# Four modulation vectors of the second layer: from TensorE inside the attention to ScalarE and GpSimd beside the long convolution

## The chip, the core and the metric

The program runs on one core of one Trainium2 chip, as one launch. The metric is the device time of that launch in microseconds (us), the median of the runs shown. A profile, taken in one further execution, gives the time of every instruction on every engine.

## The reference, cut to what matters

The program is a chain of two blocks on a sequence of 512 positions with 1024 features, all in float32. The first block has two layers; each is steered by six vectors of 1024 numbers that depend only on the input vector `c` and on one weight matrix per layer:

```
c_act = silu(c)                                        # 1024 numbers
for i in (0, 1):
    mod = c_act @ ada_w[i] + ada_b[i]                  # 1024 x 6144 weights
    sh1, sc1, g1, sh2, sc2, g2 = split(mod, 6)
    h = rms_norm(x, norm_mix_g[i]) * (1 + sc1) + sh1
    y = mla_mixer(h) if i == 0 else hyena_mixer(h)     # attention / long convolution
    x = x + g1 * y
    h = rms_norm(x, norm_ffn_g[i]) * (1 + sc2) + sh2
    x = x + g2 * hier_moe(h)                           # 16 experts, top 2
# second block: 2 x (retention, short conv, conformer conv, then a feed-forward)
```

The mixer of layer 1, `hyena_mixer`, is a projection to 3072 features with a three-tap convolution, and then twice a gate times a long convolution over the whole sequence (in the reference by FFT), and an output projection. Of layer 1's six vectors, `sh1` and `sc1` are needed before this mixer, and `g1`, `sh2`, `sc2` and `g2` only after it.

## The kernel before, in words

Features lie on the 128 partitions, positions along the free axis; a feature vector of 1024 is eight tiles. Matrix products run on TensorE at float32 accuracy as three products of split operands: a weight tile is loaded raw (128x1024, one DMA on SyncE's queue), ScalarE rounds it (`wh`, L257), VectorE takes the rest (`wl`, L258), and TensorE multiplies `wh` and `wl` with the activations, which are split in the same way. `fm` is the loop over such weight tiles; it hands back one output tile of 128x512 at a time.

The framework fixes the order of each engine's instructions before the launch; semaphores hold an instruction until its inputs are there, and behind it everything on that engine waits. The order follows the Python program, which interleaves generators by hand: `pump(gen, n)` lets a generator go n steps on. Generator `fill` makes modulation vectors as a filler inside the attention of layer 0 (a step after each stage of a head), beside a second filler, `filt`, which computes the filters of the long convolution.

One vector costs in `ada_vec` (L467): eight raw weight tiles through SyncE's queue; of each, four matmuls of 256 columns with `c_act` broadcast to 32 stationary columns, into the tile `ada` of a PSUM bank; then a copy on ScalarE (`adar`, L482), two transposes on TensorE (`adat`, L251), and the addition of the bias on VectorE (`mod`, L492). After layer 1's `sc2`, `router_prep(1)` follows, 16 small matmuls into the tile `rb`. `fill` is the chain of four vectors of layer 0 and all six of layer 1.

`hyena` (L1795) comes after layer 0's mixture of experts. Its first part has two loops over `fm` of eight tiles each. Per tile there are 24 matmuls into `acc`; ScalarE moves the bank out (`u`, L1687), VectorE convolves it (`y`, L1692 to L1694). In the first loop, each step also takes one of eight tiles computed earlier and put off (`late`): VectorE convolves that too and forms sums and differences of it (`eo`, L1700 and L1701), which TensorE transposes (`eoT`, L1704). The second part is the long convolution: `run` steps through forward transforms (`fwd_gen`: matmuls into `fu`, and VectorE multiplies them with the filter's spectrum `KK`, L1737 to L1745) and inverse transforms (`inv_gen`: matmuls into `iv`). GpSimd has no instruction in this whole stretch. In the trace, the first loop's convolutions with `eoT` lie between about 722 and 762 us, the second loop up to 808 us, then the first forward transform up to 829 us, and the pairs of inverse and forward transform after it.

Of the kernel before, what the change touches and what calls it, by code (L numbers as in the profile page):

```python
# [9 lines left out]
FT = mybir.dt.float32  # L10
# [3 lines left out]
AF = mybir.ActivationFunctionType  # L14
OP = mybir.AluOpType
# [7 lines left out]
KD = 8  # L23
# [430 lines left out]
ADA_OFF = {"sh1": 0, "sc1": 8, "g1": 16, "sh2": 24, "sc2": 32, "g2": 40}  # L454
# [6 lines left out]
class Mla:  # L461
# [7 lines left out]
    def ada_vec(self, i, nm):  # L469

        nc, W = self.nc, self.A["ada_w"]
        P = self.ps("ada") if (i, nm) == (0, "sh1") else self.fps("ada") if (i, nm) in EARLY else self.acc("ada")
        o = ADA_OFF[nm]
        for k in range(KD):
            raw = self.raw()
            nc.sync.dma_start(raw, W[i, k * 128:(k + 1) * 128, o * 128:o * 128 + 1024])
            c1 = self.cact[:, k:k + 1].to_broadcast([128, 32])
            for q in range(4):
                self.mm(P[32 * q:32 * q + 32, :256], c1, raw[:, 256 * q:256 * q + 256], k == 0, k == KD - 1)
            yield  # L480
        R = self.t("adar")
        nc.scalar.activation(R[:, :256], P[:, :256], AF.Copy)  # L482
        Q = self.ps("adat")
        self.tr4(Q, [R[:, b * 128:(b + 1) * 128] for b in range(2)])
        dst = self.mod[i][:, o:o + 8]
        nc.vector.tensor_tensor(
            dst.rearrange("p (q b) -> p q b", q=4),
            Q[:, :256].rearrange("p (b q z) -> p q b z", b=2, q=4)[:, :, :, 0],
            self.pc(f"ada_b{i}", o, 8).rearrange("p (q b) -> p q b", q=4), op=OP.add)
        for v, g in (("sc1", "gmix"), ("sc2", "gffn")):  # L490
            if v == nm:
                nc.vector.scalar_tensor_tensor(dst, dst, 1.0, self.pc(f"{g}{i}"), op0=OP.add, op1=OP.mult)  # L492
        yield

    def m_(self, i, nm, k):
        o = ADA_OFF[nm] + k
        return self.mod[i][:, o:o + 1]
# [382 lines left out]
class Moe:  # L880
# [301 lines left out]
    def moe_down(self, a, w, row, i):  # L1182
        if YT:
            for n in range(2):
                P, Y = self.acc("dn"), self.t("Y")
                self.down_mm(P, a, w, n)
                self.nc.scalar.activation(Y, P, AF.Copy)
                (self.nc.gpsimd, self.nc.sync, self.nc.scalar)[YQ].dma_start(
                    self.ys[i][row:row + 128, n * 512:(n + 1) * 512], Y)
            return  # L1190
        Y = self.p("Y", FT)
        for n in range(2):
            P = self.acc("dn")
            self.down_mm(P, a, w, n)
            self.nc.scalar.activation(Y[:, n * 512:(n + 1) * 512], P, AF.Copy)
        (self.nc.gpsimd, self.nc.sync, self.nc.scalar)[YQ].dma_start(self.ys[i][row:row + 128, :], Y)

# [360 lines left out]
class Hyena:  # L1558
# [236 lines left out]
    def hyena(self, norm, F, fill=None):  # L1795
        nc, A = self.nc, self.A
        rB = norm[1]
        W = A["hy_w_in"]
        EU = [self.new_eu(0) for _ in range(2)]
        H, late = [], []  # L1800

        def conv(ct, u, b):
            self.eo(self.hconv3(u, 16 + ct, b), EU[ct // 4], ct % 4)

        for ct, u in F.tiles(rB):
            late.append((ct, u, F.bias[:, ct:ct + 1]))
        for ct, u in F.more((2048 + 512, 2048 + 768), rB):
            late.append((ct + 4, u, F.bias[:, ct % 2:ct % 2 + 1]))
            for k in range(2):
                H.append(self.mod_split(len(H), rB, 1, "sc1", "sh1"))  # L1810
        F.R = None
        for c in range(2):
            for ct, P in self.fm(W, c * 1024, 1024, H):
                if late:
                    conv(*late.pop(0))
                nc.scalar.dma_start(self.xd[c, ct], self.hconv3(P, c * 8 + ct))
        del H
        self.tu, self.ti = ([self.table(A[n][a], f != m, f) for a in range(2)] for n, f, m in (("k_tu", FF, 3), ("k_ti", FI, 15)))
        Z = [None] * KD
        EU2 = [None, None]  # L1820

        def sink1(ct, z):
            if ct % 4 == 0:
                EU2[ct // 4] = self.new_eu(1)
            self.eo(z, EU2[ct // 4], ct % 4)

        def sink2(ct, z):
            Z[ct] = self.split_p(z, "z2")

        def run(*gs):  # L1830
            gs = list(gs)
            while gs:
                for g in list(gs):
                    if next(g, "end") == "end":
                        gs.remove(g)
        Y = [[] for _ in range(4)]
        run(self.fwd_gen(0, 0, EU[0], Y[0]))
        run(self.inv_gen(0, 0, Y[0], sink1), self.fwd_gen(0, 1, EU[1], Y[1]))
        run(self.inv_gen(0, 1, Y[1], sink1), self.fwd_gen(1, 0, EU2[0], Y[2]))
        run(self.inv_gen(1, 0, Y[2], sink2), self.fwd_gen(1, 1, EU2[1], Y[3]))  # L1840
        run(self.inv_gen(1, 1, Y[3], sink2))
        self.tu = self.ti = None
        if fill is not None:
            self.pump(fill, 1000)
        self.ex = 0
        return self.resid(A["hy_w_out"], Z, 1, "g1")

# [424 lines left out]
class Kernel(Base, Mla, Moe, Hyena, Mix):  # L2272

    def run(self):
        nc = self.nc
        self.startup()
        ada = self.ada_vec(0, "sc1")
        if XP0 == 0:
            self.x_load((nc.scalar, nc.sync, nc.gpsimd)[XQ])
        self.pump(ada, 3)  # L2280
        if XP0 == 1:
            self.x_load((nc.scalar, nc.sync, nc.gpsimd)[XQ])
        filt = self.filter_gen(*self.filter_consts(nc.scalar))
        if XP0 == 2:
            self.x_load((nc.scalar, nc.sync, nc.gpsimd)[XQ])
        self.pump(filt, 3)
        r, H = self.x_in()
        self.pump(ada, 6)
        self.rope_tables()
        self.pump(filt, 1)  # L2290
        self.moe_consts()
        self.moe_zero()
        fill = chain(self.ada(0, "g1 sh2 sc2 g2"), self.ada(1, "sh1 sc1 g1 sh2 sc2 g2"))
        out = []
        pre = self.mla_pre(r, H, out)
        n = 0
        while not out:
            n += 1
            self.pump(pre, 1)
            self.pump(filt, FP)  # L2300
            if n > FG:
                self.pump(fill, FB)
        ss = self.mla(*out.pop(), fill, filt)
        F = self.first("hyena", 1)
        norm = self.moe(0, ss, F)
        self.ex = 4
        ss = self.hyena(norm, F)
        F = self.first("mix", 0)
        self.ex = 0
        norm = self.moe(1, ss, F)  # L2310
        for l in range(2):
            F1 = self.first("ffn", l)
            self.ex = 0
            norm = self.mix(l, norm, F, F1)
            self.ex = 0
            F = None if l else self.first("mix", 1)
            norm = self.ffn(l, norm, F1, F)
# [28 lines left out]
```

## Time and profile before

| | us |
|---|---|
| median of 3 runs | 2897.11 |
| lowest, highest run | 2891.73, 2899.1 |
| the profiled execution, its own time | 2900.35 |
| its span, first to last instruction | 2898.6 |
| TensorE busy in the span | 2751.2 |
| VectorE busy | 1923.6 |
| ScalarE busy | 1290.0 |
| GpSimd busy | 228.8 |

The span is 1.75 us shorter than the time of the same execution; what lies around it is start and end of the launch. The profiled execution is 3.2 us over the median, and 1.3 us over the highest of the three runs. "Busy" counts only the time in which an instruction ran. A view by windows gives these sums for a stretch of the span; a timeline gives single instructions (start, length, engine, line, output<-inputs), and in brackets for how long the engine stood idle before it and what ended that.

### The profile page before, as it was taken

The page shows a single profiled execution, that of the slowest core. Times are in us where ns is not written, and L with a number is a line of the kernel's source. Part 1 is how long each engine was busy: PE and PEld are TensorE (multiplying, and loading weights), DVE is VectorE, ACT ScalarE, POOL GpSimd, SP SyncE. Part 2 cuts the span into 40 slices and gives each one's busy share as a digit, 9 for nine tenths or more (in the row PEclk, how much of TensorE's full clock was granted, in tenths as well). Part 3 has the DMA queues.
Part 4 walks back from the last instruction along what each step waited for, and adds up shares of the span by engine and source line. Part 5 has one row for each costly group of instructions (what it writes and reads, how often), then busy time and mean ns, then how long its engine had stood idle before and what let it go on. Part 6 is the DMA issues. An engine that isn't in the chain of part 4 may idle for free.

```text
span 2898.6 us, 37820 instructions
## 1 busy us (share of the span) xinstructions
PE 2751.2 (95%) x14240; PEld 2227.9 (77%) x14264; DVE 1923.6 (66%) x3278; ACT 1290.0 (45%) x2204; POOL 228.8 (8%) x287
## 2 busy tenths in 40 slices
PE   6899997999999799899999999999999999999998
PEld 3666776878866588778888888888878888888887
DVE  6676748987776499579835485264779645584363
ACT  4566746874312488343224353243443224353341
POOL 0111002111000111400000100001100000100001
PEclk8999998999999899899999999999999999999998
DMA  6666357972443499332232222322322322222321
GB/s 214 203 215 216 135 213 273 403 291 81 164 156 119 146 378 377 134 96 80 95 102 88 88 80 95 102 91 91 102 84 84 102 95 88 72 97 94 102 91 48
DMA packets 129173, 419.06 MB, mean 145 GB/s; under 512 B 14400, under 2 KB 24848, under 8 KB 128976
## 3 DMA queue, kind: packets, MB, share of 16 engines
q1 hardware_dynamic: 96128, 335.06, 33.3%
q0 software_dynamic: 13328, 46.68, 4.5%
q10 hardware_dynamic: 19520, 34.76, 3.5%
q8 instruction: 116, 1.90, 0.3%
q14 instruction: 81, 0.66, 0.1%
HBM read 380.78 MB, written 33.56 MB: 143 GB/s over the span
## 4 chain that ended last, share of the span: by engine, by line
PE 56%; DVE 3%; issue 3%; POOL 1%; DMA 1%; ACT 1%; POOLq 0%; DVEq 0%; ACTq 0%
PE acc L242 46%; PE f L242 3%; PE gu L242 2%; PE v L242 2%; PE dn L242 1%; PE nh L242 1%; PE o L242 1%; PE S L242 1%; DVE pre L1885 1%; DVE wl L258 0%; DMA y<-ys,pos 0%; DVE uy L1944 0%; PE bc L242 0%; PE xT L1151 0%; DVE X L258 0%
## 5 line engine op out<-in xcount | busy, mean ns | idle before, releaser
L242 PE MATMUL acc<-X,wh 128*128 128x512 f32 x2432 | 757.9, 392 | 0.8 <-ACT X L257 0.6
L258 DVE TENSOR_TENSOR wl<-raw,wh 128x1024 fp32r<-128x1024 f32 (+1 forms) x338 | 414.0, 1228 | 402.9 <-ACT wh L257 386.5
L257 ACT ACTIVATE wh<-raw 128x1024 fp32r<-128x1024 f32 (+2 forms) x362 | 370.1, 1027 | 449.8 <-PE acc L242 380.3
L242 PEld LDWEIGHTS acc<-X,wh 128*128 128x128 f32 x2432 | 456.2, 188 | 98.4 <-issue 2.0
L242 PE MATMUL acc<-X,wl 128*128 128x512 f32 x1216 | 474.6, 390 | 0.0
L242 PEld LDWEIGHTS acc<-X,wl 128*128 128x128 f32 x1216 | 229.0, 188 | 47.4
L242 PE MATMUL acc<-f,wh 128*128 128x512 f32 (+1 forms) x912 | 229.9, 352 | 0.0
L258 DVE TENSOR_TENSOR wl<-pre,wh 128x1024 fp32r<-128x1024 f32 x184 | 219.6, 1219 | 15.4 <-ACT wh L257 11.6
L257 ACT ACTIVATE wh<-pre 128x1024 fp32r<-128x1024 f32 x184 | 191.2, 1061 | 21.3 <-PE gu L242 17.3
L242 PEld LDWEIGHTS acc<-f,wh 128*128 128x128 f32 x912 | 159.5, 193 | 21.9
L2113 DVE SCALAR_TENSOR_TENSOR cfa<-sb,par,cfa 128x511 f32<-128x511 f32 (+15 forms) x240 | 163.0, 731 | 1.8 <-ACT cfa L2108 1.8
L242 PE MATMUL acc<-xr,wh 128*128 128x512 f32 x448 | 138.5, 390 | 0.6 <-DVE x L1133 0.6
L242 PE MATMUL acc<-f,wl 128*128 128x512 f32 (+1 forms) x384 | 136.7, 356 | 0.0
L72 POOL TENSOR_TENSOR sq<-sq,sq 128x256 f32<-128x256 f32 (+1 forms) x60 | 61.5, 1025 | 931.3 <-ACT sq L398 929.8
L1944 DVE SCALAR_TENSOR_TENSOR uy<-acc,par,uy 128x511 f32<-128x511 f32 (+1 forms) x128 | 95.7, 748 | 58.6 <-ACT uy L1940 56.3
L242 PE MATMUL f<-xr,wh 128*128 128x256 f32 x640 | 130.7, 299 | 4.1 <-DVE xr L261 2.2
L242 PEld LDWEIGHTS f<-xr,wh 128*128 128x128 f32 x640 | 106.6, 201 | 11.6 <-issue 5.5
L242 PE MATMUL gu<-wh,xh 128*128 128x512 f32 x264 | 112.8, 427 | 1.9 <-ACT wh L257 1.9
L242 PE MATMUL gu<-wl,xh 128*128 128x512 f32 x264 | 105.3, 399 | 1.1 <-DVE wl L258 1.1
L242 PE MATMUL gu<-wh,xl 128*128 128x512 f32 x264 | 105.8, 401 | 0.0
L242 PEld LDWEIGHTS acc<-xr,wh 128*128 128x128 f32 x448 | 83.8, 188 | 18.2 <-issue 1.1
L242 PE MATMUL f<-xr,wl 128*128 128x256 f32 x320 | 94.1, 295 | 0.0
(517 smaller groups left out, 5205.0 us busy)
## 6 DMA issues: line engine op xcount, KB each, us to landing
pre<-in_moe SPq DMA_DIRECT2D x184, 512.0 KB
raw<-in_w_in SPq DMA_DIRECT2D x106, 512.0 KB
raw<-in_ada_w SPq DMA_DIRECT2D x96, 512.0 KB
raw<-in_w_up SPq DMA_DIRECT2D x88, 512.0 KB
raw<-in_w_down SPq DMA_DIRECT2D x40, 512.0 KB
ys<-Y POOLq DMA_DIRECT2D x28, 512.0 KB
raw<-in_hy_w_in SPq DMA_DIRECT2D x22, 512.0 KB
kd<-K ACTq DMA_DIRECT2D x32, 256.0 KB
```

What stands on the lines that cost most here:

```text
L72: K.nc.gpsimd.tensor_tensor(self.a[:, cs], self.a[:, cs], q[:, cs], op=OP.add)
L242: return self.nc.tensor.matmul(o, a, b, start=st, stop=sp)
L257: nc.scalar.activation(h, src, AF.Copy)
L258: nc.vector.tensor_sub(l, src, h.bitcast(FT))
L1885: self.nc.vector.scalar_tensor_tensor(t1, self.x[k], self.pc(g, k), rB, op0=OP.mult, op1=OP.mult)
L1944: nc.vector.scalar_tensor_tensor(y[:, d:], src[:, :512 - d], taps[d], y[:, d:], op0=OP.mult, op1=OP.add)
L2113: v.scalar_tensor_tensor(c[j][:, d:], glu[i][:, :512 - d], self.pc(f"cf_conv_w{l}", (30 - d) * 4 + i), c[j][:, d:], op0=OP.mult, op1=OP.add)
```

## The change

Layer 1's `g1`, `sh2`, `sc2` and `g2` leave the filler of the attention. The new generator `ada_pool` makes them: it loads each 128x1024 tile of weights on GpSimd's own DMA queue, two steps ahead into a ring of three buffers (`avr`), multiplies it on ScalarE with the column of `c_act` that belongs to its rows (one number per partition), and adds it on GpSimd to an accumulator (`ava`). After eight tiles the accumulator holds 128 partial sums per output, and eight matmuls with a single column of ones sum them over the partitions into `adat`; VectorE adds the bias as before. That is 32 loads, 32 multiplications on ScalarE, 28 additions on GpSimd and 32 matmuls of one column in the program (each is two in the profile, since a float32 product has two passes). The generator is stepped once after each of the 16 tiles of hyena's two `fm` loops and once per round of `run`, and what is left is drained at the end. `router_prep(1)` stands behind it.

```
--- before.py
+++ after.py
@@ -491,6 +491,43 @@
             if v == nm:
                 nc.vector.scalar_tensor_tensor(dst, dst, 1.0, self.pc(f"{g}{i}"), op0=OP.add, op1=OP.mult)
         yield
+
+    def ada_pool(self, i, names):
+
+        nc, W = self.nc, self.A["ada_w"]
+        acc, names = self.p("ava", FT), names.split()
+        todo = [(o, k) for o in (ADA_OFF[nm] for nm in names) for k in range(KD)]
+        ring, L = [self.p("avr", FT) for _ in range(3)], []
+
+        def load():
+            if len(L) < len(todo):
+                o, k = todo[len(L)]
+                L.append(ring[len(L) % 3])
+                nc.gpsimd.dma_start(L[-1], W[i, k * 128:(k + 1) * 128, o * 128:o * 128 + 1024])
+        load()
+        load()
+        for n, (o, k) in enumerate(todo):
+            load()
+            c = self.cact[:, k:k + 1]
+            if k == 0:
+                nc.scalar.activation(acc, L[n], AF.Copy, scale=c)
+            else:
+                nc.scalar.activation(L[n], L[n], AF.Copy, scale=c)
+                nc.gpsimd.tensor_tensor(acc, acc, L[n], op=OP.add)
+            if k == KD - 1:
+                Q = self.ps("adat")
+                for j in range(KD):
+                    self.mm(Q[:, j:j + 1], acc[:, j * 128:(j + 1) * 128], self.ones[:, 0:1], True, True)
+                self.ada_end(i, names[n // KD], Q[:, :8])
+            yield
+
+    def ada_end(self, i, nm, Q):
+        nc, o = self.nc, ADA_OFF[nm]
+        dst = self.mod[i][:, o:o + 8]
+        nc.vector.tensor_tensor(dst, Q, self.pc(f"ada_b{i}", o, 8), op=OP.add)
+        for v, g in (("sc1", "gmix"), ("sc2", "gffn")):
+            if v == nm:
+                nc.vector.scalar_tensor_tensor(dst, dst, 1.0, self.pc(f"{g}{i}"), op0=OP.add, op1=OP.mult)
 
     def m_(self, i, nm, k):
         o = ADA_OFF[nm] + k
@@ -1814,6 +1851,7 @@
                 if late:
                     conv(*late.pop(0))
                 nc.scalar.dma_start(self.xd[c, ct], self.hconv3(P, c * 8 + ct))
+                self.pump(fill, 1)
         del H
         self.tu, self.ti = ([self.table(A[n][a], f != m, f) for a in range(2)] for n, f, m in (("k_tu", FF, 3), ("k_ti", FI, 15)))
         Z = [None] * KD
@@ -1833,6 +1871,7 @@
                 for g in list(gs):
                     if next(g, "end") == "end":
                         gs.remove(g)
+                self.pump(fill, 1)
         Y = [[] for _ in range(4)]
         run(self.fwd_gen(0, 0, EU[0], Y[0]))
         run(self.inv_gen(0, 0, Y[0], sink1), self.fwd_gen(0, 1, EU[1], Y[1]))
@@ -1840,8 +1879,8 @@
         run(self.inv_gen(1, 0, Y[2], sink2), self.fwd_gen(1, 1, EU2[1], Y[3]))
         run(self.inv_gen(1, 1, Y[3], sink2))
         self.tu = self.ti = None
-        if fill is not None:
-            self.pump(fill, 1000)
+        self.pump(fill, 1000)
+        self.router_prep(1)
         self.ex = 0
         return self.resid(A["hy_w_out"], Z, 1, "g1")
 
@@ -2290,7 +2329,7 @@
         self.pump(filt, 1)
         self.moe_consts()
         self.moe_zero()
-        fill = chain(self.ada(0, "g1 sh2 sc2 g2"), self.ada(1, "sh1 sc1 g1 sh2 sc2 g2"))
+        fill = chain(self.ada(0, "g1 sh2 sc2 g2"), self.ada(1, "sh1 sc1"))
         out = []
         pre = self.mla_pre(r, H, out)
         n = 0
@@ -2304,7 +2343,7 @@
         F = self.first("hyena", 1)
         norm = self.moe(0, ss, F)
         self.ex = 4
-        ss = self.hyena(norm, F)
+        ss = self.hyena(norm, F, self.ada_pool(1, "g1 sh2 sc2 g2"))
         F = self.first("mix", 0)
         self.ex = 0
         norm = self.moe(1, ss, F)
```

On TensorE, in the middle of the attention (`S` scores, `o` and `w` a head's output and its projection, `kt` the second filler), the rows before are:

```order
L251 MATMUL adat_2525<-par,adar_2523 128x128 x2
L251 MATMUL pT_2563<-par,e_2489 128x128 x4
L242 MATMUL ada_2604<-raw_2605,cact 32x256 x4
L242 MATMUL ada_2604<-raw_2611,cact 32x256
L242 MATMUL w_2552<-HS_308,wh_2539 128x512 x2
L242 MATMUL ada_2604<-raw_2611,cact 32x256 x3
L242 MATMUL o_2618<-ph_2471,v_1788 128x256
L242 MATMUL ada_2604<-raw_2684,cact 32x256 x4
```

and now, from the same instruction on:

```order
L251 MATMUL adat_2525<-par,adar_2523 128x128 x2
L251 MATMUL pT_2563<-par,e_2489 128x128 x4
L242 MATMUL S_2629<-K_2340,Q_2279 128x512 x3
L242 MATMUL S_2629<-KP_1403,QP_2280 128x512
L242 MATMUL w_2552<-HS_308,wh_2539 128x512 x2
L242 MATMUL o_2605<-ph_2471,v_1788 128x256
L242 MATMUL S_2629<-KP_1403,QP_2280 128x512
L242 MATMUL kt_2719<-eo_1728,wh_598 128x256
```

The first vector that is moved begins at `ada_2604`; from there on the attention's own matmuls and the other filler stand next to each other.

On GpSimd, behind layer 0's mixture of experts (`sq` and `rh` belong to a norm), the rows before are the following, of which the last two already belong to layer 1's mixture of experts:

```order
L72 TENSOR_TENSOR sq_7950<-sq_7950,sq_8089 128x256
L344 TENSOR_TENSOR rh_8144<-vh_8142,mhalf 128x2
L344 TENSOR_TENSOR r_10184<-v_10182,mhalf 128x4
L1413 COPY ovx_10357<-iotas 128x1
```

and now:

```order
L72 TENSOR_TENSOR sq_7718<-sq_7718,sq_7857 128x256
L344 TENSOR_TENSOR rh_7912<-vh_7910,mhalf 128x2
L506 DMA avr_8205<-in_ada_w 128x1024
L506 DMA avr_8206<-in_ada_w 128x1024
L506 DMA avr_8207<-in_ada_w 128x1024
L506 DMA avr_8205<-in_ada_w 128x1024
L516 TENSOR_TENSOR ava_8204<-ava_8204,avr_8206 128x1024
L506 DMA avr_8206<-in_ada_w 128x1024
L516 TENSOR_TENSOR ava_8204<-ava_8204,avr_8207 128x1024
```

An addition and the load that reuses its buffer alternate from here through the whole of hyena.

On TensorE, at the last `eoT` of hyena's first loop (`acc` is the projection), the rows now are:

```order
L1741 MATMUL eoT_8581<-par,eo_8578 128x128 [waits DVE_49,PE_49,Activation_49]
L1741 MATMUL eoT_8581<-par,eo_8578 128x128
L242 MATMUL adat_8598<-ones,ava_8204 128x1 [waits PE_49,Activation_49,Pool_49]
L242 MATMUL adat_8598<-ones,ava_8204 128x1 x3
L1741 MATMUL eoT_8581<-par,eo_8578 128x128 [waits DVE_49]
L1741 MATMUL eoT_8581<-par,eo_8578 128x128
L242 MATMUL adat_8598<-ones,ava_8204 128x1 x4
L242 MATMUL acc_8620<-h_7991,wh_8610 128x512 x2
```

The eight one-column matmuls of the first vector are new here; the other rows and their distances are those of before, as is VectorE's order but for four additions of the bias.

## Rows read from the trace of the kernel before

**Rows 1.** First part of the page, busy us by engine, whole span.

```profile
PE 2751.2 (95%) x14240; PEld 2227.9 (77%) x14264; DVE 1923.6 (66%) x3278; ACT 1290.0 (45%) x2204; POOL 228.8 (8%) x287
```

**Rows 2.** Windows in the attention: stretch, us; busy us (count) by engine; clock, DMA.

```profile
150.00:200.00 50.00, 43.96 (x326) 31.26 (x320) 34.07 (x100) 31.66 (x98) 5.80 (x7) 0.97 0.63 216
225.00:325.00 100.00, 94.52 (x703) 67.42 (x702) 68.77 (x204) 66.20 (x220) 13.63 (x16) 0.98 0.59 200
325.00:350.00 25.00, 23.82 (x155) 20.19 (x153) 21.72 (x58) 21.34 (x48) 0.00 (x0) 1.00 0.34 121
```

**Rows 3.** Tile `ada` alone, the four moved vectors: PE, PEld, ACT busy.

```profile
231.90:324.00 92.10, 22.67 (x256) 7.86 (x256) 1.20 (x3) 0.98 0.57 193
```

**Rows 4.** Groups by line, PE, 225 to 325: busy us, mean ns | idle.

```profile
L251 PE MATMUL adat<-par,adar 128*128 128x128 f32 x8 | 1.9, 330 | 0.4 <-ACT adar L482 0.4
...
L242 PE MATMUL rb<-par,mod 128*128 128x32 f32 x16 | 1.9, 271 | 0.0
```

**Rows 5.** Windows in hyena, same columns as the second group.

```profile
722.00:762.00 40.00, 39.88 (x188) 32.10 (x188) 37.73 (x62) 16.39 (x28) 0.00 (x0) 1.00 0.42 148
762.00:808.00 46.00, 46.00 (x199) 37.05 (x198) 24.04 (x32) 11.89 (x17) 0.00 (x0) 1.00 0.52 181
808.00:829.00 21.00, 21.00 (x65) 11.98 (x64) 17.72 (x30) 0.38 (x1) 0.00 (x0) 1.00 0.77 275
829.00:867.00 38.00, 37.13 (x140) 24.14 (x139) 32.12 (x61) 4.89 (x15) 0.00 (x0) 1.00 0.29 90
```

**Rows 6.** Chain of waits, one-column matmuls elsewhere: start us, us.

```profile
1291.99 0.97 PE st L242 x8
```

**Rows 7.** Timeline of GpSimd near 1992: start us, us.

```profile
1992.17 1.81 POOL L72 TENSOR_TENSOR sq<-sq,sq 128x512 f32<-128x512 f32 x1 [301.80 <-ACT sq L398]
1997.81 1.28 POOL L72 TENSOR_TENSOR sq<-sq,sq 128x512 f32<-128x512 f32 x1 [3.83 <-ACT sq L398]
```

**Rows 8.** Timeline of VectorE near 1992.

```profile
1991.60 1.23 DVE L258 TENSOR_TENSOR wl<-raw,wh 128x1024 fp32r<-128x1024 f32 x1 [0.76 <-ACT wh L257]
1993.07 1.99 DVE L258 TENSOR_TENSOR wl<-raw,wh 128x1024 fp32r<-128x1024 f32 x1 [0.24 <-ACT wh L257]
```

**Rows 9.** Timeline of GpSimd near 682.

```profile
682.56 0.74 POOL L72 TENSOR_TENSOR sq<-sq,sq 128x256 f32<-128x256 f32 x1 [4.76 <-ACT sq L398]
```

**Rows 10.** Timeline of VectorE near 683.

```profile
682.85 0.73 DVE L261 SCALAR_TENSOR_TENSOR xr<-x,mod,xr 128x256 fp32r<-128x256 f32 x1 [0.55 <-ACT xr L260]
...
683.84 0.47 DVE L261 SCALAR_TENSOR_TENSOR xr<-x,mod,xr 128x256 fp32r<-128x256 f32 x1
```

**Rows 11.** Timeline of GpSimd near 1202.

```profile
1201.75 1.60 POOL L72 TENSOR_TENSOR sq<-sq,sq 128x256 f32<-128x256 f32 x2 [7.73 <-ACT sq L398]
```

**Rows 12.** Timeline of VectorE near 1202.

```profile
1201.36 0.48 DVE L1133 SCALAR_TENSOR_TENSOR x<-cT,mod,x 128x256 f32<-128x256 f32 x1 [0.21 <-PE cT L242]
...
1202.68 0.47 DVE L1133 SCALAR_TENSOR_TENSOR x<-cT,mod,x 128x256 f32<-128x256 f32 x1
```

**Rows 13.** Timeline of VectorE in the first fm loop.

```profile
737.22 0.42 DVE L1701 TENSOR_TENSOR eo<-y 128x256 f32<-128x256 f32 x1
```

**Rows 14.** Timeline of PE in the first fm loop.

```profile
737.70 0.60 PE L1704 MATMUL eoT<-par,eo 128*128 128x128 f32 x4
```

**Rows 15.** Groups by line, VectorE, 700 to 815.

```profile
L258 DVE TENSOR_TENSOR wl<-raw,wh 128x1024 fp32r<-128x1024 f32 x17 | 20.8, 1223 | 7.6 <-ACT wh L257 7.6
...
L1693 DVE SCALAR_TENSOR_TENSOR y<-u,par,y 128x511 f32<-128x511 f32 x16 | 12.0, 748 | 0.3
L1692 DVE TENSOR_SCALAR y<-u,par 128x512 f32<-128x512 f32 x16 | 8.7, 545 | 16.3 <-ACT u L1687 16.3
```

**Rows 16.** Groups by line, VectorE, 815 to 905.

```profile
L1742 DVE TENSOR_TENSOR y<-ya,yb 128x512 f32<-128x512 f32 x14 | 9.5, 679 | 0.0
L1738 DVE TENSOR_TENSOR yb<-fu,KK 128x512 f32<-128x512 f32 x14 | 9.5, 679 | 0.0
```

**Rows 17.** Timeline of ScalarE, a 128x1024 product by a column.

```profile
633.90 1.15 ACT L1489 ACTIVATE y<-y,M 128x1024 f32<-128x1024 f32 x1
```

## The prediction

> **What bounds the kernel now.** I read the page's first part first: TensorE is busy 95% of the span, VectorE 66%, ScalarE 45%, GpSimd 8% [rows 1]. An average cannot price this change, which takes from one stage and adds to another, so next came windows of both. In the attention, 225 to 325 us, where the moved vectors run, TensorE is busy 94.52 of 100 us; the 25 us that follow, with no filler of vectors left, have 23.82 of 25 [rows 2]. VectorE (68.77 and 21.72 us) and ScalarE (66.20 and 21.34) have room in both. In hyena TensorE is full throughout: 39.88 of 40 us in the first loop, 46.00 of 46 in the second, 21.00 of 21 in the first forward transform, 37.13 of 38 after it [rows 5]. VectorE differs by stage: 37.73 of 40 in the first loop, 24.04 of 46 in the second, then 17.72 of 21 and 32.12 of 38. ScalarE has half of it free, and GpSimd does nothing. So one stage gives back what TensorE no longer does, and in the other TensorE has no gap, and VectorE has one in the second loop only.
>
> **What goes from the attention.** A view of the tile `ada` alone shows 256 records, 22.67 us: 32 tiles by four matmuls by two passes, exactly the four vectors [rows 3]. Their eight records of `adat` take 1.9 us and go too; 16 of `rb`, 1.9 us, move behind hyena [rows 4]. That is 26.5 us of busy time. From 225 to 350 us TensorE is busy 94.52 + 23.82 = 118.34 of 125 us; 91.8 remain. How long they last is a choice of busy share. At 0.953, as without filler, 91.8 take 96.4 us and 28.6 are gained. At 0.88, as at 150 to 200 us [rows 2], they take 104.4 and 20.6 are gained; I set the lower end at 19. A filler also covers waits, and without it the remaining matmuls come closer to what they wait for. VectorE's 90.5 and ScalarE's 87.5 us fit into 100. I take a share of 0.91, between the two rows: **-24 us** (-28 to -19).
>
> **What TensorE gets in hyena.** Each vector ends with eight one-column matmuls, two records each: 64 records. Where such matmuls stand in the chain, eight take 0.97 us [rows 6], so 64 take 7.8; `rb` adds its 1.9. TensorE has no gap to hide them in: **+9.7 us** (8 to 9.7).
>
> **What the additions on GpSimd cost.** They are 28, of 128x1024. GpSimd's additions took 0.74 us for 256 columns and 1.28 for 512 [rows 7, 9]; continued along that line, 1024 columns are an estimate of 2.4 us. They are no load on TensorE by themselves. The question is VectorE. At 1992 us both engines overlap: a `wl` takes 1.23 us undisturbed, a GpSimd addition started at 1992.17 takes 1.81 instead of 1.28, and the next `wl`, started at 1993.07 while the addition still ran, takes 1.99 [rows 7, 8]. Each waited for the other. At 682.85 an `xr` takes 0.73 instead of 0.47, beside an addition started at 682.56 [rows 9, 10]. Against that, an instruction of VectorE that reads one input from PSUM took 0.47 us beside GpSimd additions and 0.48 without [rows 11, 12]. So two SBUF inputs are held until a running addition has ended; with one in PSUM they are not.
>
> The Trainium skill ("SBUF — State Buffer", section "Who interferes with whom") says the same more sharply: the pair of ports that the two engines share is an exclusive lock, whoever issues first keeps it for the whole instruction, and a VectorE instruction with two SBUF inputs contends with a GpSimd instruction that reads SBUF. The trace agrees (1.99 against 1.23 us). By this rule the change comes out slower as summed below; without it, faster, as in the first rival.
>
> In the first loop most of VectorE's work has two SBUF inputs: `wl` at 1223 ns, the taps (L1693, L1694) at 748 ns; `y` of L1692, at 545 ns, has one [rows 15]. The order places the seven multiplications, and with them the seven additions, of the first vector in this loop; the load that refills a buffer stands behind the addition that used it. When an addition has the lock, VectorE's next instruction waits up to 2.2 us of its 2.4; with the short one-input ones in between I take 2.0, so 14 us, of which VectorE's own 2.3 us idle absorb 2. TensorE has no reserve there: an `eo` that ends at 737.64 releases an `eoT` that starts at 737.70 [rows 13, 14], and all eight `eoT` of the loop start within 0.3 us of their `eo`'s end. **+12 us** (0 to 15).
>
> The other 21 additions meet more room. In the second loop VectorE is busy 24 of 46 us, so seven additions are hidden but for **+1** (0 to 4). In the first forward transform four products of six read PSUM (as L1738) and two, such as L1742, don't [rows 16]; nothing of the inverse is there yet to cover a late one. By the order seven additions lie in it; half of their 2.0 us is **+7** (0 to 15). After it VectorE has 5.9 us of 38 free; seven by 1.7, the shorter products holding less, is 12, less the 5.9 that is free and a rest that the one-column matmuls overlap: **+5** (0 to 9). What VectorE is late while TensorE works on the one-column matmuls counts once: **-1**.
>
> ScalarE gets 32 products of 128x1024 by a column, 1.15 us each [rows 17], 37 us in 140 where it is busy 34 [rows 5]: 0 (to 3), hidden behind TensorE; without that cover, an in-order ScalarE that waits for a load would hold `wh` and `u`. The 32 loads leave SyncE's queue, 17 MB, and come back on GpSimd's, in windows at 148 to 275 GB/s: 0 (to 4). Four buffers fewer for split weights in hyena: 0, since weights are split a tile ahead of use there and `wl` waits for `wh`, not for buffers [rows 15].
>
> **Sum.** -24 + 9.7 + 12 + 1 + 7 + 5 - 1 = **+9.7 us**. Against the profiled execution, 2900.35, that is 2910.0; its time is 3.2 above the median, within what runs differ by, so against the median of 2897.11 it is **2907 us**.
>
> **Rivals.** First: VectorE is not held, or its held time is hidden, because GpSimd gives way instead (its own 1.81 for 1.28 shows that it waits too). Then -24 + 9.7 + 2 = -12: 2885 us. Against it speak 1.99 and 0.73 us. Second: half of the hold is absorbed, since the additions fall into the one-input instructions or into idle time. The 25 us of hold become 12.5, and the sum is -24 + 9.7 + 12.5 = -2: 2895 us, no difference. Third: the attention gains only 15 to 19, because waits that the filler covered open up: 2912 to 2916 us. Fourth: the ring becomes the bound. A load can start only when its buffer's addition is done, and ScalarE's product stands in order before `wh` and `u`. If a load takes longer than the three steps ahead of it, some 7 us, ScalarE waits, then TensorE; at about half a microsecond for each of 25 products that is +13 on the sum: 2920 us. The windows' DMA share of 0.42 to 0.77 [rows 5] leaves room, which speaks against it.
>
> **How the numbers follow.** What a measurement here can tell from no change is 0.3%, 8.7 us: no change is 2888.4 to 2905.8. My forecast has 0.37, with its own range from 2899 to 2916, and is partly within 0.3%. The first rival has 0.22, the second 0.22, the third 0.07, the fourth 0.12. The range reaches from 2884, so that the first rival is nearly in it, to 2921. Faster: the first rival, 0.22. Same: the second and a good fifth of the forecast, 0.30. Slower: the rest, 0.48.
>
> **What would show it.** In the attention, the scores and projections between 225 and 350 us end some 24 us earlier, and TensorE's share there stays over 0.9. In hyena's first loop VectorE's groups of `wl` and taps have a mean well above 1223 and 748 ns, its busy time comes to the window's length, and TensorE has new waits for `eo`, `u` or `wl`. The additions on GpSimd last over 2.4 us. The one-column matmuls total near 7.8 us. I am wrong if `wl` keeps 1223 ns beside the additions (first rival), if VectorE is held but TensorE doesn't wait (second), if the attention gains under 19 (third), or if ScalarE waits for `avr` loads for longer than a microsecond at a time (fourth).

## The result, and the profile after

The changed kernel takes 2928.68 us (median of 4 runs, 2926.74 to 2934.83) against 2897.81 (2891.73 to 2899.1): a ratio of 1.0112, 95% interval 1.0098 to 1.0126. It is slower, as forecast, but by 31 us and not by 9.7, and outside the range that ended at 2921. The first part of its page:

```profile
PE 2744.9 (94%) x14064; PEld 2228.4 (76%) x14064; DVE 1966.7 (67%) x3278; ACT 1322.1 (45%) x2232; POOL 316.2 (11%) x347
```

VectorE is busy 43 us more than in [rows 1], with the same number of instructions, 3278; TensorE is busy 6 us less in a span 28 us longer.

**The attention** gave back less than half of what was forecast. The tile `gu` opens layer 0's mixture of experts; its row has the least, median and greatest duration in ns, and then its first and last start in us; first the kernel before, then the changed one:

```profile
L242 PE MATMUL gu<-wh,xh x264: 387/393/775, 458.9 to 1155.6; 128*128 128x512 f32 x132
```

```profile
L242 PE MATMUL gu<-wh,xh x264: 387/393/776, 447.7 to 1191.4; 128*128 128x512 f32 x132
```

Its start moved from 458.9 to 447.7, 11.2 us. That is one pair of traces: in the eleven traces whose attention is that of the changed kernel, the start lies between 445.3 and 454.2, so the gain is known to between 5 and 14 us only. What stands between is in windows of the changed kernel (columns as in [rows 2]), the stretch without the vectors and two parts of it:

```profile
222.00:340.00 118.00, 100.37 (x599) 81.23 (x597) 89.99 (x261) 88.48 (x273) 13.81 (x16) 0.97 0.17 57
260.00:280.00 20.00, 15.71 (x85) 12.95 (x84) 14.91 (x39) 13.28 (x42) 1.70 (x2) 0.91 0.19 62
300.00:320.00 20.00, 16.05 (x93) 13.36 (x92) 16.90 (x48) 14.23 (x42) 2.18 (x3) 0.91 0.23 79
```

TensorE's share is 0.85, below the 0.88 that I took as the low row, and in two parts the granted clock is 0.91.

**Hyena** grew from 214.6 us (first projection matmul to first of the output projection) to 261.3. Both stretches as windows, first the kernel before, then the changed one, which answers to [rows 5]:

```profile
713.30:927.90 214.60, 208.79 (x833) 151.10 (x832) 163.06 (x274) 48.33 (x89) 0.00 (x0) 0.99 0.39 133
```

```profile
701.10:962.40 261.30, 229.13 (x914) 164.69 (x912) 209.47 (x281) 82.82 (x121) 86.64 (x57) 0.93 0.50 167
```

VectorE is busy 46 us more, TensorE 20, and TensorE's idle time went from 5.8 to 32.2 us. Only some 8 of TensorE's 20 are new work: with the same matmuls e11 below has it busy 217.10 us at a granted clock of 0.99, where it is 229.13 at 0.93 here. The first loop in detail, VectorE's timeline and under it GpSimd's and TensorE's:

```profile
722.07 3.03 DVE L1729 TENSOR_SCALAR y<-u,par 128x512 f32<-128x512 f32 x1
725.02 0.53 DVE L1729 TENSOR_SCALAR y<-fu,par 128x512 f32<-128x512 f32 x1
725.48 3.17 DVE L1730 SCALAR_TENSOR_TENSOR y<-u,par,y 128x511 f32<-128x511 f32 x1
728.57 3.29 DVE L1730 SCALAR_TENSOR_TENSOR y<-fu,par,y 128x511 f32<-128x511 f32 x1
731.79 0.74 DVE L1731 SCALAR_TENSOR_TENSOR y<-u,par,y 128x511 f32<-128x511 f32 x1
...
734.25 2.55 DVE L1737 TENSOR_TENSOR eo<-y 128x256 f32<-128x256 f32 x1
```

```profile
722.40 2.41 POOL L516 TENSOR_TENSOR ava<-ava,avr 128x1024 f32<-128x1024 f32 x1
...
725.70 2.40 POOL L516 TENSOR_TENSOR ava<-ava,avr 128x1024 f32<-128x1024 f32 x1
...
728.96 2.35 POOL L516 TENSOR_TENSOR ava<-ava,avr 128x1024 f32<-128x1024 f32 x1
...
734.17 2.35 POOL L516 TENSOR_TENSOR ava<-ava,avr 128x1024 f32<-128x1024 f32 x1 [2.01 <-ACT avr L515]
```

```profile
736.95 1.09 PE L1741 MATMUL eoT<-par,eo 128*128 128x128 f32 x4 [9.29 <-DVE eo L1737]
```

The addition of 722.40 takes 2.41 us, and VectorE's `y` of L1729, 0.54 us alone, takes 3.03 until it has ended; the taps of L1730 behind it take 3.17 and 3.29 (0.74 alone) beside the additions of 725.70 and 728.96. Their neighbours, with no addition running, are at 0.53 and 0.74. TensorE waits 9.29 us for the `eo` behind them. When it starts, the clock is at 0.50, the level of 1.2 GHz, and the four `eoT` take 1.09 us; in [rows 14] four took 0.60. Two windows of that stretch:

```profile
720.00:730.00 10.00, 5.87 (x27) 4.43 (x26) 10.00 (x6) 4.02 (x5) 9.05 (x7) 1.00 0.51 148
730.00:740.00 10.00, 3.05 (x10) 2.60 (x11) 10.00 (x12) 3.65 (x6) 4.76 (x4) 0.50 0.72 220
```

VectorE counts as busy in all of it. The sum of TensorE's waits for `eo`, and then of ScalarE's for loads (total, number, longest), over hyena:

```profile
PE eoT L1741 <- DVE eo L1737: 20.6, 6, 9.3
```

```profile
ACT avr L515 <- DMA avr<-in_ada_w: 32.1, 13, 8.3
```

The second is a wait that the forecast had left out of its sum: ScalarE, which works in order, stood 32.1 us before products whose load had not landed. How much of it TensorE paid is left to the experiments.

### The profile page after: what moved, and what is told of

It is laid out like the page before. It is cut to its first block, busy times and chain, and to the rows that moved or that the text cites. A ratio compares the mean times of both kernels' runs of the same rounds, so it can differ in the third digit from the quotient of the medians.

```text
span 2927.0 us, 37500 instructions
## 1 busy us (share of the span) xinstructions
PE 2744.9 (94%) x14064; PEld 2228.4 (76%) x14064; DVE 1966.7 (67%) x3278; ACT 1322.1 (45%) x2232; POOL 316.2 (11%) x347
## 4 chain that ended last, share of the span: by engine, by line
PE 58%; DVE 3%; issue 1%; POOL 1%; ACT 1%; DMA 0%; POOLq 0%; DVEq 0%; ACTq 0%
PE acc L242 46%; PE gu L242 3%; PE f L242 3%; PE v L242 1%; PE dn L242 1%; PE nh L242 1%; PE o L242 1%; PE xT L1188 1%; DVE pre L1924 0%; PE S L242 0%; DMA y<-ys,pos 0%; DVE uy L1983 0%; DVE wl L258 0%; PE bc L242 0%; DVE X L258 0%
## 5 line engine op out<-in xcount | busy, mean ns | idle before, releaser
L242 PEld LDWEIGHTS f<-xr,wh 128*128 128x128 f32 x640 | 105.3, 199 | 11.1 <-issue 5.0
```

Source lines behind the costliest of these rows:

```text
L242: return self.nc.tensor.matmul(o, a, b, start=st, stop=sp)
```

## The experiments

The theories: **hold** (GpSimd's additions hold VectorE, and TensorE waits for VectorE), **loads** (they land late, and what stands behind them on an engine waits), and **gaps** (the attention's matmuls are chains, and without the filler TensorE waits in them). Since executions of one kernel differ by some 10 us here, the stretch of hyena in each trace is compared beside the times; it is 214.6 to 216.5 us in the four kernels whose hyena makes no vectors (before, e1, e6, e13), and 257.7 in e16, whose hyena is that of the changed kernel with its 261.3. A difference of a few us between two such stretches is therefore not shown. Ratios are to the kernel before, on the same chip, with a 95% interval.

**e1_none.** The four vectors are left out but for their bias, hyena's matmuls for them too:

```
-                nc.gpsimd.dma_start(L[-1], W[i, k * 128:(k + 1) * 128, o * 128:o * 128 + 1024])
...
-                nc.scalar.activation(acc, L[n], AF.Copy, scale=c)
...
-                nc.gpsimd.tensor_tensor(acc, acc, L[n], op=OP.add)
...
-        nc.vector.tensor_tensor(dst, Q, self.pc(f"ada_b{i}", o, 8), op=OP.add)
+        nc.vector.tensor_scalar(dst, self.pc(f"ada_b{i}", o, 8), 1.0, None, op0=OP.mult)
```

> The four vectors are left out (each is only its bias), in the attention and in hyena; the small matmuls of the router's preparation stay behind hyena. It shows what the attention alone gives back. If the prediction's share of 0.91 held there: about -24 +1.9 = -22 us against before (2876). If, as the trace of the changed kernel reads (its last score 12.9 us earlier, the mixture of experts 11.2 us earlier), the filler had covered waits: -9 to -11 us (2887 to 2889), TensorE busy 0.85 of the stretch from 222 to 340 us, and hyena as long as before.

2893.34 us, ratio 0.9982 (0.9965 to 0.9998). The mixture of experts starts at 445.3 for 458.9, hyena is as long as before, and from 222 to 340 us TensorE is busy 101.12 of 118 us, 0.86:

```profile
222.00:340.00 118.00, 101.12 (x591) 82.85 (x590) 89.44 (x257) 87.88 (x268) 13.81 (x16) 0.96 0.16 52
699.90:914.50 214.60, 209.84 (x849) 152.73 (x848) 163.43 (x276) 48.30 (x89) 0.00 (x0) 0.99 0.39 133
```

The second reading holds for TensorE's share and for hyena; the time fell by less than its 9 to 11 us. The attention, freed of 26.5 us of TensorE's work, gives 14 us in this trace, 11 in the changed kernel's, and 5 in the times (0.5 to 10 by the interval).

**e2_no_adds.** `nc.gpsimd.tensor_tensor(acc, acc, L[n], op=OP.add)` deleted.

> As the changed kernel, but GpSimd's 28 additions are left out (the loads, ScalarE's products, the one-column matmuls stay). If GpSimd's additions hold VectorE, nearly all of the loss in hyena beyond the one-column matmuls goes: -12 + 9.7 = -2 us against before, 2893 to 2899, and VectorE's taps and wl are back at 0.75 and 1.22 us. If the loss comes from the loads (ScalarE waiting for them, traffic), it stays at 2915 or more.

2926.78 us, 1.009 (1.0058 to 1.0122): a miss for the hold as the only cause. But nothing held VectorE (taps 748 ns, `wl` 1222), and ScalarE waited 85.3 us for loads, not 32.1: without the additions, the products of the next vector were put ahead of its first one, which kept one buffer of three. The edit had made the loads worse while it took the hold away.

**e3_no_loads.** The line with `nc.gpsimd.dma_start` deleted, the ring filled with zeros once.

> As the changed kernel, but the 32 loads are left out (the ring holds zeros); products, additions and one-column matmuls stay. If the additions hold VectorE, it stays within 8 us of the changed kernel, 2920 to 2930. If the loads are the cause, it falls to about 2897.

2930.38 us, 1.011 (1.0068 to 1.0152), and hyena's stretch is 258.3 us:

```profile
700.20:958.50 258.30, 229.23 (x914) 165.22 (x912) 208.07 (x281) 83.44 (x121) 75.40 (x28) 0.93 0.33 110
```

Nearly the whole loss is there without a load.

**e4_adds_dve.** `nc.vector.tensor_tensor` in place of `nc.gpsimd.tensor_tensor` for the addition.

> As the changed kernel, but VectorE makes the 28 additions itself, 28 x 1.22 = 34 us of its own time, and nothing holds it. If the hold is the cause, a share of these 34 us shows, less than the 43 us by which VectorE's busy time grew: some 20 to 25 us, sum -12 + 9.7 + 22 = +20, about 2915, below the changed kernel. If the loads are the cause, it is no faster than the changed kernel, 2928 or more.

2917.45 us, 1.0064 (1.0044 to 1.0084), as the hold expects. The group of the additions and the stretch:

```profile
L516 DVE TENSOR_TENSOR ava<-ava,avr 128x1024 f32<-128x1024 f32 x28 | 34.1, 1217 | 3.6 <-ACT avr L515 3.1 <-ACT ava L513 0.4
```

```profile
702.30:943.20 240.90, 224.90 (x913) 163.98 (x912) 193.42 (x309) 82.24 (x121) 15.75 (x29) 0.96 0.54 181
```

VectorE's own 34.1 us for the same 28 additions cost less than GpSimd's, which held it for 46. That 2915 came out is in part luck: the 22 us were put down to VectorE's additions, but the stretch is only 1.5 us longer than in e8, which has none; the rest is what e10 and e8 find in the products and the loads.

**e8_no_adds.** The sums are left out: each product goes to `acc` itself, so that the order of e2 doesn't arise:

```
-                nc.scalar.activation(L[n], L[n], AF.Copy, scale=c)
-                nc.gpsimd.tensor_tensor(acc, acc, L[n], op=OP.add)
+                nc.scalar.activation(acc, L[n], AF.Copy, scale=c)
```

> As the changed kernel, but each of ScalarE's products is written to the accumulator itself, so that GpSimd's 28 additions are gone while the products keep their order (with e2_no_adds they moved ahead, and only two of three buffers were left to the loads). If GpSimd's additions are what costs in hyena: attention -12, one-column matmuls +9.7, about 2896 (2890 to 2902). If the loads alone cost as much: 2915 or more, with ScalarE waiting for loads before products that TensorE needs.

2909.22 us, 1.0053 (1.0037 to 1.007): between the two. The additions are worth some 17 us of the 31; about 14 above before are left.

```profile
699.50:938.90 239.40, 222.72 (x914) 162.80 (x913) 163.72 (x281) 83.28 (x121) 15.40 (x29) 0.97 0.53 182
```

**e10_no_loads_no_adds** (e8 without the loads) and **e11_adat_alone** (e1 with the one-column matmuls):

> As e8_no_adds, but the 32 loads are left out too (the ring holds zeros): ScalarE's 32 products, the one-column matmuls and the router's matmuls stay. If e8_no_adds lost its 15 us in hyena beyond the 9.7 of TensorE's new work to loads for which ScalarE waits in order: hyena from its first projection matmul to the first of the output projection lasts 214.6 + 10 = 225 us (239.4 with the loads), and the time is 2890 to 2898. If the products or the one-column matmuls themselves cost them: 239 us again, and 2905 to 2912.

> As e1_none, with only the 32 one-column matmuls per launch (on an accumulator of zeros) and the router's matmuls at the changed kernel's places; no loads, products or additions. By the prediction's price, 7.8 + 1.9 us: hyena's stretch is 214.6 + 9.7 = 224 us. If a fall of the granted clock or waits behind them cost more than their records last: 230 us or more.

2901.34 us, 1.0023 (1.0013 to 1.0034), and 2900.35, 1.0015 (0.9998 to 1.0031). The stretches, first e10, then e11:

```profile
704.00:934.40 230.40, 221.81 (x913) 161.90 (x911) 163.79 (x281) 83.45 (x121) 0.00 (x0) 0.97 0.37 123
```

```profile
701.80:924.70 222.90, 217.10 (x913) 159.94 (x912) 163.95 (x281) 48.38 (x89) 0.00 (x0) 0.99 0.38 128
```

So hyena grows 214.6, 222.9, 230.4, 239.4, 261.3: one-column and router matmuls +8.3, ScalarE's products +7.5, loads +9.0, additions +21.9. e11 is as expected; e10 is longer than its 225 and above its 2898. The steps hold in this order only, since loads and additions overlap: with the additions there, loads are worth 3 us (e3 to the changed kernel), and without loads the additions are worth 27.9 (e10 to e3). The products' step is the least sure: the times of e11 and e10 differ by 1.0 us. Where in hyena the additions cost is in its four parts, up to the first `adat`, the rest of the second loop, the first forward transform and what follows; first e8, then the changed kernel:

```profile
699.50:751.50 52.00, 49.49 (x223) 39.73 (x223) 46.41 (x77) 27.74 (x41) 4.32 (x8) 0.97 0.61 208
751.50:798.70 47.20, 47.20 (x228) 39.69 (x226) 22.16 (x30) 21.33 (x25) 4.22 (x8) 1.00 0.77 261
798.70:812.60 13.90, 13.90 (x35) 6.25 (x35) 11.27 (x19) 5.75 (x5) 2.11 (x4) 1.00 0.86 307
812.60:938.90 126.30, 112.13 (x434) 77.14 (x432) 83.89 (x157) 28.46 (x51) 4.75 (x9) 0.96 0.37 129
```

```profile
701.10:764.20 63.10, 49.74 (x225) 39.67 (x223) 60.20 (x77) 30.39 (x43) 24.93 (x15) 0.92 0.53 171
764.20:811.40 47.20, 47.20 (x229) 39.67 (x227) 34.61 (x30) 20.22 (x25) 21.46 (x15) 1.00 0.74 256
811.40:826.40 15.00, 14.07 (x35) 6.07 (x35) 14.72 (x17) 3.79 (x4) 10.04 (x8) 1.00 0.94 330
826.40:962.40 136.00, 118.12 (x434) 79.28 (x432) 99.94 (x158) 28.42 (x51) 30.21 (x20) 0.91 0.35 116
```

That is +11.1, 0, +1.1 and +9.7 us.

**e15_ring6.** e8 with six buffers and five loads ahead.

> As e8_no_adds, with a ring of six buffers and five loads ahead. If its 9 us over e10_no_loads_no_adds come from ScalarE, which waits in order for loads that come late (28.7 us of such waits in e8_no_adds): the waits go, and hyena's stretch falls from 239.4 to about 231 us, the time to 2898 to 2903. If they come from the traffic itself: 239 us again, about 2909.

2896.61 us, 0.9996 (0.9984 to 1.0009), a little below the first reading's 2898, and a stretch of 227.7:

```profile
704.40:932.10 227.70, 221.26 (x912) 162.67 (x912) 163.48 (x281) 83.47 (x121) 13.72 (x26) 0.97 0.53 188
```

ScalarE's waits for loads, first in e8, then here:

```profile
ACT ava L512 <- DMA avr<-in_ada_w: 28.7, 13, 5.6
```

```profile
ACT ava L512 <- DMA avr<-in_ada_w: 4.0, 2, 2.7
```

With them went the loads' whole cost, at the same DMA share of 0.53 as in e8. It was lateness, not traffic.

**e5_memset2.** e8 with two `nc.gpsimd.memset(L[n], 0.0)` where an addition stood.

> As e8_no_adds, but in place of each addition GpSimd fills the buffer twice with zeros, 2 x 0.95 us, which only writes. If a GpSimd instruction holds VectorE only when it reads SBUF: VectorE's taps and wl keep 0.75 and 1.22 us, and the time is within 5 us of e8_no_adds. If any GpSimd instruction on SBUF holds it: 28 x 1.9 = 53 us of hold at most, and 2920 or more.

2909.05 us, 1.0037 (1.0024 to 1.0049), as e8. GpSimd worked 53.3 us; two groups of VectorE:

```profile
L1729 DVE SCALAR_TENSOR_TENSOR y<-u,par,y 128x511 f32<-128x511 f32 x16 | 11.9, 746 | 0.3
...
L1728 DVE TENSOR_SCALAR y<-fu,par 128x512 f32<-128x512 f32 x8 | 7.1, 889 | 0.0
```

The taps keep their 746 ns, but the one-input `y<-fu` goes from 542 to 889 (and `y<-u` from 545 to 686): a write alone holds that form, and not the two-input ones.

**e7_pe_hyena.** `self.ada(1, "g1 sh2 sc2 g2")` handed to `hyena` for `ada_pool`.

> The four vectors are made in hyena, at the changed kernel's places, but by TensorE as before (128 matmuls of 256 columns, transposes), through SyncE's queue; nothing on GpSimd. TensorE is full there, so its 26.5 us show in full against the -12 of the attention: +14 us, 2912 (2906 to 2918), VectorE not held. It is then 15 us below the changed kernel, which would say that GpSimd's way costs more than the matmuls that it was to save. If hyena cannot take loads or ScalarE's copies either, 2925 or more.

2926.45 us, 1.0111 (1.0093 to 1.0128): as slow as the changed kernel, a miss by 14. TensorE's 26.5 us do show (busy 235.54 in a stretch of 250.6), and the weights in SyncE's queue delay hyena's own loads (2.7 us of this wait in the kernel before):

```profile
DVE ya L1774 <- DMA KK<-kd: 20.9, 5, 5.6
```

**e6_none_fr2, e13_before_fr2, e16_after_fr2.** In e1, in the kernel before and in the changed one, the filters' filler gets more of the attention: `-FR_ = 3`, `+FR_ = 2`.

> As e1_none (vectors left out), but the other filler of the attention, the filters, gets a step every second stage and not every third. If the attention without the vectors' matmuls is left with gaps because nothing fills them, work that now lies behind the attention moves into them: TensorE's busy share from 222 to 340 us rises from 0.85 to 0.90 or more, and it is 5 to 9 us below e1_none. If the gaps are chains that no filler reaches: the same as e1_none within 2 us.

> The kernel before, with only the filters' step every second stage, to tell how much of e6_none_fr2 and of e12_two_in_loop2 is owed to this alone. TensorE is busy 0.945 of the attention from 225 to 325 us, so little is left to fill: 2892 to 2898. If it gains more than 6 us, the filters' pace was a loss in the kernel before too.

> The changed kernel itself, with only the filters' step every second stage. If the forecast -24 of the attention was missed because nothing filled the gaps that the vectors left: the mixture of experts starts 7 to 10 us earlier than in the changed kernel (447.7), and the time is 2914 to 2922 for 2928.7. If e6_none_fr2's gain came from elsewhere: 2928 again.

2876.28 us, 0.9941 (0.9919 to 0.9962); 2901.59, 1.0019 (1.0005 to 1.0032), above its 2898; 2920.02, 1.0078 (1.0058 to 1.0098), as expected. By the ratios e6 is 12 us below e1, more than its 5 to 9. In e6 TensorE is busy 0.905 of 222 to 340 us:

```profile
222.00:340.00 118.00, 106.79 (x648) 89.60 (x647) 97.54 (x282) 90.63 (x278) 14.11 (x16) 0.94 0.20 64
```

The mixture of experts starts at 437.7 in e6 (445.3 in e1) and at 438.3 in e16 (447.7 in the changed kernel). In the kernel before, where the vectors fill the gaps, the pace gains nothing. So the attention's missing 12 us were gaps, and most of them could be filled: in e6 the last `kt` starts 12 us earlier than in e1, at 364.5, although the last score starts 13 us later, at 341.8. What the filters' tile `kt` takes of TensorE, from 325 to 350 us before, and from 222 to 325 us in the changed kernel and in e6:

```profile
325.00:350.00 25.00, 3.50 (x24) 3.11 (x24) 1.50 (x4) 0.78 (x2) 1.00 0.34 121
```

```profile
222.00:325.00 103.00, 9.31 (x60) 8.24 (x60) 3.35 (x9) 1.96 (x5) 0.97 0.17 60
```

```profile
222.00:325.00 103.00, 14.73 (x95) 12.71 (x93) 6.17 (x16) 3.37 (x8) 0.93 0.22 71
```

**e12_two_in_loop2.** `g1` and `g2` alone go through `ada_pool`: `self.pump(fill, 2 if c else ct == 6)` in the `fm` loops, `FR_ = 2`.

> A version to beat both: two vectors (g1, g2) go the changed kernel's way, but only in hyena's second loop, two steps per tile, where VectorE has 22 of 46 us free; sh2 and sc2 stay on TensorE in the attention, and the filters get a step every second stage. If the hold costs only where VectorE has no slack: the second loop stays within 2 us of 46 plus 4 us of one-column matmuls, half of the vectors' attention time is saved, 2885 to 2893, below before. If a hold shows there too, or the additions run over into the forward transform: 2898 to 2905.

2917.35 us, 1.0072 (1.0053 to 1.0092), a miss. The order put the products earlier than the loop that steps them; the first additions ran at 745 to 760 us, where VectorE still had the first loop's work, and TensorE waited 9.7 us for `eo` there and later 5.1 us for the second accumulator. A window from the start of that stretch:

```profile
740.00:750.00 10.00, 8.42 (x39) 6.39 (x37) 9.17 (x10) 6.56 (x9) 5.12 (x4) 1.00 0.59 193
```

**e14_fused_dve.** One instruction on VectorE for product and sum (for the first product of a vector a `tensor_scalar`), ring of six, `FR_ = 2`:

```
+                nc.vector.scalar_tensor_tensor(acc, L[n], c, acc, op0=OP.mult, op1=OP.add)
```

> A version to beat both: product and sum in one VectorE instruction (weights times the column plus the accumulator, 32 of them), nothing on ScalarE or GpSimd but the loads, five loads ahead in a ring of six, and the filters' step every second stage. From the runs so far: attention -12 and another -8 to -14 by the filters' pace; in hyena +8.3 for the one-column matmuls (e11), none of the 7.5 of the products (e10), at most 9 for loads (e8), and 2 to 6 for VectorE's 32 x 1.4 = 45 us, of which e4_adds_dve showed 34 to be nearly free. Sum -20 + 8 + 4 + 4 = -4: 2887 to 2896 beside 2896 of before. If VectorE's own 45 us, or its in-order waits for loads, cost as much as GpSimd's hold: 2910 or more.

2889.26 us (12 runs), 0.9979 (0.9966 to 0.9992): as expected, and faster than the kernel before by 0.2%. The interval leaves out 1, but 0.2% is under the 0.3% that the prediction asks of a difference. Its 28 multiply-adds:

```profile
L515 DVE SCALAR_TENSOR_TENSOR ava<-avr,cact,ava 128x1024 f32<-128x1024 f32 x28 | 35.7, 1276 | 0.0
```

Hyena's stretch is 231.9, and the mixture of experts starts at 438.8.

## Why the prediction was wrong

Its sign was right, and so was the mechanism on which it rested, the hold; three terms of the sum were too small, all to the same side. The step that failed by most is the share of 0.91 in the attention; then come the loads and the products, both taken as hidden.

- *"I take a share of 0.91, between the two rows: -24 us."* It was 0.85, and some 11 us in the traces (5 in the times of e1). My third rival, at 15 to 19, was still too mild. I read the stretch with no filler of vectors, 325 to 350 us [rows 2], as the attention without its filler. But the other filler was denser there: `kt` took 14% of TensorE's time, and in the changed kernel from 222 to 325 us 9%. In e6 it took 14% of that stretch too, and TensorE's share in it rose from 0.85 to 0.89; the rest to 0.95 stays open.
- *"TensorE gets +9.7"*: 8.3 in e11. Right.
- *The additions*, +12 +1 +7 +5 -1 = 24: 21.9 from e8 to the changed kernel. Right in kind: taps at 1172 and 1247 ns, PSUM readers such as L1775 at 678. Right in place for the two loops, 13 for 11.1. That the sum is right is luck behind them: the first forward transform, where four additions began and not seven, cost 1.1 and not 7, and what follows 9.7 and not 5. Wrong too is that the one-input `y` is free: it is held as well (1016 ns for 545).
- *"ScalarE gets 32 products ... 0 (to 3), hidden behind TensorE"*: 7.5 from e11 to e10 in the stretch, but 1.0 in the times. (The windows of [rows 5] last 145 us together, not 140.) The products stand in order before `u`, `wh` and `zc`, so free time on the engine need not make them free. TensorE's idle time grew by 2.8 us only, and its busy time by 4.7, at a granted clock of 0.97 for 0.99; that the products' place in the order did this is argued, not shown.
- *The loads, "0 (to 4)"*: 9.0, by ScalarE's waits, and none with a deeper ring. That was my fourth rival's mechanism, at +13, to which I gave 0.12 as an alternative; it came beside the hold.

By the traces' terms the sum is -11.2 + 8.3 + 7.5 + 9.0 + 21.9 = +35.5, against 28.4 in the profiled spans and 31 in the medians. Of the difference, 1.0 lies between the first `gu` and hyena, and 6.1 after hyena, which lasts 1964.6 us to the end for 1970.7. Nothing in the change reaches there except `g2`, and it is no more than that stretch varies by: it lasts 1963.4 to 1972.6 us in the 17 traces, 1972.6 in e1, which leaves the vectors out, and 1970.8 in e15, which has loads and products. So these 6.1 us lie within the spread of the traces.

## What to carry to other kernels

Price a filler that is taken away by what then fills its gaps, not by its busy time. An idle engine is a free place only if its instructions neither hold a busy engine nor wait in order ahead of others: for the same additions, VectorE with 34.1 us of its own time gave a stretch of 240.9 us, and an otherwise idle GpSimd 261.3. Effects that were set up as rivals may add up, so a range needs their sum as well.

## What the runs showed of the hardware

A GpSimd addition of 128x1024 took 2.36 us in the median (1217 ns on VectorE) and held the VectorE instruction that met it until its end, 3.29 us for 0.74 at worst. It was held itself too: the one that began at 717.02 us took 4.50. The records do not settle the prediction's "whoever issues first": the tap of 725.48 us was held by the addition of 725.70, but a record shows a start and not an issue. The Trainium skill ("SBUF — State Buffer", section "Who interferes with whom") says that an instruction with two SBUF inputs contends with a GpSimd instruction that reads and not with one that only writes, and that `tensor_scalar` can enter a mode that takes both ports and contends as well. The runs agree with both: beside memsets the taps kept 746 ns, and the `tensor_scalar` of L1728 took 889 for 542. Unexpected was how TensorE's waits are paid a second time: after 9.29 us of waiting the granted clock was 0.50, and over hyena it was 0.93 for the 0.99 of e11, with 12 us more of busy time for the same matmuls.
